# Decay matrices in place and whole head pairs in one matmul group: a state-space layer on one Trainium2 core

## The chip, the core and the metric

The kernel runs on one core of one Trainium2 chip. The time is device microseconds of that core for one execution of the whole kernel; lower is better. Engines are named as in the profile: PE multiplies matrices, DVE, ACT and POOL work elementwise, SP issues the DMAs.

## The reference

A trunk of two layers, each a feed-forward half step, a token mixer and another half step, for 512 tokens of width 1024. The change is in the mixer of the first layer, a bidirectional state-space scan in chunks (here of 128 tokens):

```python
def ssd_chunked(X, dt, A, Bm, Cm):
    Xc = (X * dt[..., None]).reshape(b, c, CHUNK, g, j, p)
    a_cs = jnp.cumsum(a, axis=-1)
    L = jnp.exp(segsum(a))
    CB = jnp.einsum('bclgn,bcsgn->bgcls', Cc, Bc)
    y_diag = jnp.einsum('bgcls,bgjcls,bcsgjp->bclgjp', CB, L, Xc)
    ...
    states = jnp.einsum('bgjzc,bcgjpn->bzgjpn', chunk_decay, states)[:, :-1]
    y_off = jnp.einsum('bclgn,bcgjpn,bgjcl->bclgjp', Cc, states, jnp.exp(a_cs))
    return (y_diag + y_off).reshape(b, t, h, p)
```

`mamba2_bidir` runs it forward and on the flipped sequence, adds both, gates with SiLU(z), normalizes by group and projects out. There are 32 heads of width 64 in 4 groups of 8 heads. In the matrix `CB * L` the forward scan fills the lower triangle and the backward scan the upper one, and the diagonal gets both.

## The kernel before

All activations lie as channels x tokens, 128 channels by 512 tokens to a tile. Float32 products of projections are split in a high and a low part (`split`: ACT makes the high part at L123, DVE the low part at L124), and three matmuls make one product (`mm3`, L166). A projection of one column tile takes 24 such matmuls of 128x512 and is called a unit here. Its 512 KB of weights come through `load` (L99), issued by SP into a ring of 4 tiles.

The state-space stage `ssm` works through four head groups. `dt_chain` computes the decay rows and writes them to a scratch array `scr` in DRAM. For a group, `prepare` makes transposes, the products CB of the two token halves (`cbs`, 256 tokens each) and the states between halves. A group has four head pairs. For a pair:

- `ssd_head`, once for a head, reads that head's decay rows of both directions into a tile `rw` (512 KB written, L744) and the decay towards the other half into `ch` (256 KB, L746). DVE multiplies `ch` by C (L747), and POOL masks the diagonal blocks by selects (L761), in `rw` in place and into `dx`.
- `ssd_mats`, for a head and a token half c, makes a decay matrix: ACT's exponentials (L769 to L772), POOL's add of the second diagonal part (L775) and DVE's product with CB (L776). The result is a tile `E` of 128x512, out of a ring of five.
- `ssd_out`, for the pair and a token half, multiplies: six matmuls of 64 columns x 256 tokens (L786) into one PSUM tile `mid`. The profile records each as two.

Between them stands the list `todo`: projections of the next group (B, C, x, z), and the output projections of the last group (`outp`). The loop runs over eight steps s, two for a pair, and does an eighth of `todo` after each. `silu` applies all SiLUs of the next group together, since each change of ACT's function set loads a table. `gated_norm` of the last group runs in two parts.

The order in which the instructions stand on each engine isn't the program's: a scheduler puts them by its own estimates of when inputs are there and buffers come free. Each engine then runs its own list strictly in order, and waits for what the head of its list needs; this holds for SP's DMAs too.

## Time and profile before

| | |
|---|---|
| Three runs | 2184.02, 2176.71 and 2184.0 us, median 2184.0 |
| Profiled execution | 2180.44 us, span 2178.6 us |
| PE busy | 2121.8 us (97%) |
| DVE busy | 1778.6 us (82%) |
| ACT busy | 1095.2 us (50%) |
| POOL busy | 155.3 us (7%) |
| Granted PE clock, mean | 0.99 |

A line of the profile names source line, engine, operation and tiles (`out<-in`); `acc`, `mid` and `ln` are PSUM tiles. In timelines the first number is the start in microseconds from the span's start, the second the duration, and a bracket at the end gives the idle time of the engine before the instruction and who ended it. In tables by stretch there stand the stretch, its length, the busy time of PE, PE's weight loads, DVE, ACT and POOL with counts, and then the granted clock, the DMA share and the GB/s. A busy PE isn't PE at its peak. The stage of the change lies between 400 and 790 us.

### The profile page before, as it was taken

The page shows a single profiled execution, that of the slowest core. Times are in us where ns is not written, and L with a number is a line of the kernel's source. Part 1 is how long each engine was busy: PE and PEld are TensorE (multiplying, and loading weights), DVE is VectorE, ACT ScalarE, POOL GpSimd, SP SyncE. Part 2 cuts the span into 40 slices and gives each one's busy share as a digit, 9 for nine tenths or more (in the row PEclk, how much of TensorE's full clock was granted, in tenths as well). Part 3 has the DMA queues.
Part 4 walks back from the last instruction along what each step waited for, and adds up shares of the span by engine and source line. Part 5 has one row for each costly group of instructions (what it writes and reads, how often), then busy time and mean ns, then how long its engine had stood idle before and what let it go on. Part 6 is the DMA issues. An engine that isn't in the chain of part 4 may idle for free.

```text
span 2178.6 us, 34176 instructions
## 1 busy us (share of the span) xinstructions
PE 2121.8 (97%) x13182; PEld 1861.4 (85%) x13182; DVE 1778.6 (82%) x3096; ACT 1095.2 (50%) x1830; POOL 155.3 (7%) x258
## 2 busy tenths in 40 slices
PE   7999999999999989999999999999999989999998
PEld 6889899866777778999999989899888878989897
DVE  6979899556766689989889998987877879859697
ACT  4424354767655547434356434343866647424353
POOL 0000000044232300000000000000111100000000
PEclk9999999999999999999999999999999999999999
DMA  9863644564535413545443273723322221323231
GB/s 322 301 212 121 219 134 152 127 178 137 158 122 155 121 68 131 198 147 196 162 136 106 98 252 104 256 91 111 98 81 78 66 78 68 125 70 116 86 110 39
DMA packets 90083, 301.19 MB, mean 138 GB/s; under 512 B 10048, under 2 KB 13504, under 8 KB 89920
## 3 DMA queue, kind: packets, MB, share of 16 engines
q1 hardware_dynamic: 88384, 294.81, 40.8%
q0 software_dynamic: 1536, 4.20, 0.9%
q8 instruction: 103, 1.69, 0.3%
q14 instruction: 60, 0.49, 0.1%
HBM read 289.53 MB, written 5.24 MB: 135 GB/s over the span
## 4 chain that ended last, share of the span: by engine, by line
PE 80%; DVE 8%; ACT 4%; issue 4%; POOL 2%; DMA 2%; POOLq 0%; ACTq 0%; SPq 0%; DVEq 0%
PE acc L166 65%; PE mid L166 9%; PE mid L786 1%; PE mid L948 1%; POOL E L775 1%; DVE raw L184 1%; PE ln L166 1%; DMA raw<-in_adaw 1%; DMA raw<-in_wdn 1%; DVE resid L320 1%; DMA raw<-in_wgu 1%; POOL dx L761 1%; PE ln L734 1%; PE ln L970 1%; DVE lo L154 0%
## 5 line engine op out<-in xcount | busy, mean ns | idle before, releaser
L166 PE MATMUL acc<-hi,wh 128*128 128x256 f32 (+1 forms) x1584 | 530.6, 336 | 9.9 <-DVE resid L370 8.7
L166 PE MATMUL acc<-hi,wl 128*128 128x256 f32 (+1 forms) x1584 | 530.5, 335 | 0.0
L166 PE MATMUL acc<-lo,wh 128*128 128x256 f32 (+1 forms) x1584 | 529.1, 335 | 0.0
L166 PE MATMUL acc<-uh,wh 128*128 128x256 f32 (+1 forms) x1160 | 391.5, 338 | 0.3 <-ACT wh L123 0.3
L166 PE MATMUL acc<-ul,wh 128*128 128x256 f32 (+1 forms) x1160 | 389.9, 336 | 0.0
L166 PE MATMUL acc<-uh,wl 128*128 128x256 f32 (+1 forms) x1160 | 389.0, 336 | 0.0
L123 ACT ACTIVATE wh<-raw 128x1024 fp32r<-128x1024 f32 (+1 forms) x210 | 212.9, 1022 | 274.0 <-DMA raw<-in_wdn 94.2
L166 PEld LDWEIGHTS acc<-hi,wh 128*128 128x128 f32 x1584 | 300.2, 190 | 46.1 <-DVE resid L370 8.3
L453 ACT ACTIVATE wh<-raw 128x1024 fp32r<-128x1024 f32 x198 | 208.8, 1059 | 256.2 <-DVE raw L463 117.8
L166 PEld LDWEIGHTS acc<-lo,wh 128*128 128x128 f32 x1584 | 300.4, 190 | 30.7 <-DVE lo L154 1.0
L166 PEld LDWEIGHTS acc<-hi,wl 128*128 128x128 f32 x1584 | 300.4, 190 | 30.1 <-issue 0.5
L124 DVE TENSOR_TENSOR wl<-raw,wh 128x1024 fp32r<-128x1024 f32 (+1 forms) x210 | 248.9, 1186 | 47.9 <-ACT wh L123 46.5
L454 DVE TENSOR_TENSOR wl<-raw,wh 128x1024 fp32r<-128x1024 f32 x198 | 241.1, 1222 | 40.2 <-ACT wh L453 39.2
L166 PEld LDWEIGHTS acc<-uh,wh 128*128 128x128 f32 x1160 | 219.3, 189 | 29.4 <-issue 6.6
L166 PEld LDWEIGHTS acc<-ul,wh 128*128 128x128 f32 x1160 | 219.4, 189 | 24.7 <-issue 3.2
L166 PEld LDWEIGHTS acc<-uh,wl 128*128 128x128 f32 x1160 | 219.3, 189 | 23.8 <-issue 2.4
L463 DVE TENSOR_TENSOR raw<-raw 128x512 f32<-128x512 f32 x264 | 181.6, 690 | 4.9
L184 DVE SCALAR_TENSOR_TENSOR raw<-raw,cond 128x1024 f32<-128x1024 f32 x144 | 174.3, 1221 | 9.6 <-DMA raw<-in_adaw 9.3
L370 DVE SCALAR_TENSOR_TENSOR resid<-acc,gv,resid 128x512 f32<-128x512 f32 (+1 forms) x172 | 112.8, 662 | 57.5 <-PE acc L166 57.3
L316 POOL TENSOR_TENSOR rr<-vr,mhalf 128x2 f32<-128x2 f32 x12 | 8.4, 697 | 1523.4 <-DVE vr L312 1523.4
L166 PE MATMUL mid<-uh,wh 128*128 128x256 f32 (+2 forms) x332 | 99.7, 301 | 0.1
L166 PE MATMUL mid<-ul,wh 128*128 128x256 f32 (+2 forms) x332 | 99.3, 300 | 0.0
(266 smaller groups left out, 3943.4 us busy)
## 6 DMA issues: line engine op xcount, KB each, us to landing
raw<-in_wgu SPq DMA_DIRECT2D x176, 512.0 KB, 4.0
raw<-in_adaw SPq DMA_DIRECT2D x144, 512.0 KB, 4.8
raw<-in_wdn SPq DMA_DIRECT2D x64, 448.0 KB, 4.1
raw<-in_win SPq DMA_DIRECT2D x40, 512.0 KB, 3.9
raw<-in_wdn SPq DMA_DIRECT2D x32, 512.0 KB, 4.5
rw<-scr SPq DMA_DIRECT2D x32, 512.0 KB, 5.4
ch<-scr SPq DMA_DIRECT2D x32, 256.0 KB, 3.6
raw<-in_wso SPq DMA_DIRECT2D x16, 512.0 KB, 3.3
```

Source lines behind the costliest of these rows:

```text
L123: nc.scalar.activation(hi[:, :n], raw, AF.Copy)
L124: nc.vector.tensor_tensor(out=lo[:, :n], in0=raw, in1=hi[:, :n].bitcast(F32), op=ALU.subtract)
L166: last = nc.tensor.matmul(o, lhsT=a, rhs=b, start=start and j == 0, stop=j == n - 1, skip_group_check=not start)
L184: nc.vector.scalar_tensor_tensor(out=raw, in0=raw, scalar=1.0, in1=cond, op0=ALU.mult, op1=ALU.mult, accum_out=mods[l][:, j : j + 1],)
L320: nc.vector.tensor_tensor(out=t, in0=t, in1=mb, op=ALU.subtract)
L370: nc.vector.scalar_tensor_tensor(out=res[d][:, a:b], in0=pd[:, a:b], scalar=gvec[n][:, d : d + 1], in1=res[d][:, a:b], op0=ALU.mult, op1=A ...
L453: nc.scalar.activation(x[0], r, AF.Copy)
L454: nc.vector.tensor_tensor(out=x[1], in0=r, in1=x[0].bitcast(F32), op=ALU.subtract)
L463: nc.vector.tensor_tensor(out=o, in0=x, in1=y, op=ALU.add)
L734: nc.tensor.matmul(pst, lhsT=bt[:, i * P : (i + 1) * P], rhs=xd, start=o == 0, stop=o == 1)
L761: nc.gpsimd.affine_select(out=o, in_=i_, pattern=[[0, 2], [sg, P]], compare_op=ALU.is_ge, fill=-1.0e30, base=0, channel_multiplier=-sg,)
L775: nc.gpsimd.tensor_tensor(out=dg, in0=dg, in1=dx[:, c], op=ALU.add)
```

## The change

Three things change. First, the `E` tiles go: exponentials, add and product work in place in `rw`, of which there are six now instead of two, and `fetch` reads the rows of a pair one pair ahead of its use. `ch` stays at three tiles. Second, the loop runs over the four pairs: both token halves' matrices of both heads are made, then a quarter of `todo` runs, then the SiLUs if they are due, and only then `ssd_out` multiplies all of the pair, 12 matmuls in one group. Third, `prepare` of the next group comes behind the last pair's products.

```diff
-NE = 5
+NRW = 6
...
-            e1, e2, e3 = (ep.tile([P, T], F32, tag="E", name="E", bufs=NE) for _ in range(3))
+            e12, e3 = (ep.tile([P, 2, T], F32, tag="rw", name="ew", bufs=NRW) for _ in range(2))
+            e1, e2, e3 = e12[:, 0, :], e12[:, 1, :], e3[:, 0, :]
...
+        rows_of = {}
+
+        def fetch(ft):
+            if ft >= 16:
+                return
+            for h in (2 * ft, 2 * ft + 1):
+                rw = ep.tile([P, 2, T], F32, tag="rw", name="rw", bufs=NRW)
+                nc.sync.dma_start(rw, scr[:, h].unsqueeze(1)[:, :, 0:2].broadcast_to([16, 8, 2, T]))
+                rows_of[h] = rw
+
         def ssd_head(h, Ct):
-            src = scr[:, h].unsqueeze(1)
-            rw = ep.tile([P, 2, T], F32, tag="rw", name="rw")
-            nc.sync.dma_start(rw, src[:, :, 0:2].broadcast_to([16, 8, 2, T]))
+            rw = rows_of.pop(h)
             ch = ep.tile([P, T], F32, tag="ch", name="ch", bufs=3)
...
         def ssd_mats(h, c, rw, dx, cbs):
-            E = ep.tile([P, T], F32, tag="E", name="E", bufs=NE)
-            i = 2 * c
-            nc.scalar.activation(E[:, :W], rw[:, 0, c * W : (c + 1) * W], AF.Exp, bias=bias[:, i, h : h + 1])
-            nc.scalar.activation(E[:, W:], rw[:, 1, c * W : (c + 1) * W], AF.Exp, bias=bias[:, i + 1, 32 + h : 33 + h])
+            i, cc = 2 * c, slice(c * W, (c + 1) * W)
+            nc.scalar.activation(rw[:, 0, cc], rw[:, 0, cc], AF.Exp, bias=bias[:, i, h : h + 1])
+            nc.scalar.activation(rw[:, 1, cc], rw[:, 1, cc], AF.Exp, bias=bias[:, i + 1, 32 + h : 33 + h])
...
-            dg = E.rearrange("p (k q) -> p k q", k=4)[:, 0:4:3, :]
+            dg = rw.rearrange("p d (k q) -> p (d k) q", k=4)[:, i : i + 6 : 5, :]
             nc.gpsimd.tensor_tensor(out=dg, in0=dg, in1=dx[:, c], op=ALU.add)
-            nc.vector.tensor_tensor(out=E, in0=E, in1=cbs[c], op=ALU.mult)
-            return E
-
-        def ssd_out(pr_, c, py, mats, chs, xt, states):
-            cc = slice(c * W, (c + 1) * W)
+            E = rw[:, :, cc]
+            nc.vector.tensor_tensor(out=E, in0=E, in1=cbs[c].rearrange("p (k q) -> p k q", k=2), op=ALU.mult)
+
+        def ssd_out(pr_, heads, py, xt, states):
             col = [slice(pr_ * P + hh * 64, pr_ * P + (hh + 1) * 64) for hh in range(2)]
-            for k in range(3):
-                for hh in range(2):
...
+            for c in range(2):
+                cc = slice(c * W, (c + 1) * W)
+                for k in range(3):
+                    for hh in range(2):
+                        rw, ch, _ = heads[hh]
+                        lhs = xt[2 * c + k][:, col[hh]] if k < 2 else states[1 - c][:, col[hh]]
+                        rhs = rw[:, k, cc] if k < 2 else ch[:, cc]
+                        nc.tensor.matmul(py[hh * 64 : (hh + 1) * 64, cc], lhsT=lhs, rhs=rhs, start=k == 0, stop=k == 2)
...
         run(units_x(0, xs)[2:])
+        fetch(0)
...
-            for s in range(8):
-                pr_, c = divmod(s, 2)
+            for pr_ in range(4):
                 ft = g * 4 + pr_
-                if c == 0:
-                    heads = [ssd_head(ft * 2 + hh, Ct) for hh in range(2)]
-                    py = acc("mid")
-                mats = [ssd_mats(ft * 2 + hh, c, heads[hh][0], heads[hh][2], cbs) for hh in range(2)]
-                ssd_out(pr_, c, py, mats, [hd[1] for hd in heads], xt, states)
...
+                fetch(ft + 1)
+                heads = [ssd_head(ft * 2 + hh, Ct) for hh in range(2)]
+                for c in range(2):
+                    for hh in range(2):
+                        ssd_mats(ft * 2 + hh, c, heads[hh][0], heads[hh][2], cbs)
...
-                while done < tot - (2 if g == NG - 1 else 0) and done < (s + 1) * tot // 8:
+                while done < tot - (2 if g == NG - 1 else 0) and done < (pr_ + 1) * tot // 4:
                     todo[done]()
                     done += 1
-                if done >= len(first) and not batched and (s >= 6 or done == tot):
+                if done >= len(first) and not batched:
                     batched = True
                     silu(zs[g] + nbc + nxs)
-                    if g < NG - 1:
-                        cur = prepare(g + 1, nxs, nbc)
+                py = acc("mid")
+                ssd_out(pr_, heads, py, xt, states)
+                nc.vector.scalar_tensor_tensor(
+                    out=xs[pr_], in0=xs[pr_], scalar=pc(C_D + ft), in1=py, op0=ALU.mult, op1=ALU.add
+                )
+            if g < NG - 1:
+                cur = prepare(g + 1, nxs, nbc)
```

The scheduler then puts much in another order. Three places show it; numbers behind names tell buffers apart. On PE, at the first head pair of group 0, before (`mid_4382` is pair 0, `acc_4705` a projection):

```order
L786 MATMUL mid_4382<-E_4438,xt_4339 64x256
L786 MATMUL mid_4382<-E_4445,xt_4339 64x256
L786 MATMUL mid_4382<-ch_4348,st_4321 64x256
L786 MATMUL mid_4382<-ch_4366,st_4321 64x256
L166 MATMUL acc_4705<-uh_3631,wh_4701 128x512
L166 MATMUL acc_4705<-ul_3632,wh_4701 128x512
```

On PE at the same place now (`mid_4479` is pair 0, `mid_4623` pair 1):

```order
L796 MATMUL mid_4479<-ch_4353,st_4324 64x256
L796 MATMUL mid_4479<-ch_4369,st_4324 64x256
L796 MATMUL mid_4623<-rw_4349,xt_4309 64x256
L796 MATMUL mid_4623<-rw_4351,xt_4309 64x256
L796 MATMUL mid_4623<-rw_4349,xt_4319 64x256
L796 MATMUL mid_4623<-rw_4351,xt_4319 64x256
```

Behind pair 0 a projection stood; now pair 1 follows at once, since the projections of pairs 0 and 1 have both moved ahead of pair 0's group. On POOL, the adds of pair 1 before (`E_4531` to `E_4593`) and what stands around them:

```order
L761 AFFINE_SELECT rw_4512<-rw_4512 128x2x128 x2
L761 AFFINE_SELECT dx_4517<-rw_4512 128x2x128 x2
L775 TENSOR_TENSOR E_4531<-E_4531,dx_4499 128x2x128
L775 TENSOR_TENSOR E_4538<-E_4538,dx_4517 128x2x128
L775 TENSOR_TENSOR E_4586<-E_4586,dx_4499 128x2x128
L775 TENSOR_TENSOR E_4593<-E_4593,dx_4517 128x2x128
L761 AFFINE_SELECT rw_4642<-rw_4642 128x2x128 x2
```

On POOL now, the adds of pair 1 (`rw_4349`, `rw_4351`; `rw_4493` is pair 2's and `rw_4637` pair 3's):

```order
L783 TENSOR_TENSOR rw_4349<-rw_4349,dx_4500 128x2x128
L783 TENSOR_TENSOR rw_4351<-rw_4351,dx_4516 128x2x128
L783 TENSOR_TENSOR rw_4349<-rw_4349,dx_4500 128x2x128
L770 AFFINE_SELECT dx_4644<-rw_4493 128x2x128 x2
L770 AFFINE_SELECT rw_4637<-rw_4637 128x2x128 x2
L783 TENSOR_TENSOR rw_4351<-rw_4351,dx_4516 128x2x128
```

The selects of the next pair stood behind all four adds; now the last add stands behind selects of pairs 2 and 3, and `rw_4637` lies in the buffer that pair 0's matrices leave. On ACT, in the preparation of group 2, before (`xt` are the transposed copies, `rw_5941` and `rw_6130` rows of pairs fetched earlier):

```order
L727 ACTIVATE xt_5794<-ln_5789 128x512
L769 ACTIVATE E_6046<-rw_5941,ssbias_3771 128x256
L770 ACTIVATE E_6046<-rw_5941,ssbias_3771 128x256
L769 ACTIVATE E_6167<-rw_6130,ssbias_3771 128x256
L770 ACTIVATE E_6167<-rw_6130,ssbias_3771 128x256
L771 ACTIVATE dx_6135<-dx_6135,ssbias_3771 128x128
L772 ACTIVATE dx_6135<-dx_6135,ssbias_3771 128x128
```

On ACT at the same place now (`rw_6097` and `rw_6099` are the rows of pair 10, two pairs ahead):

```order
L728 ACTIVATE xt_5854<-ln_5849 128x512
L778 ACTIVATE rw_6097<-rw_6097,ssbias_3771 128x256
L728 ACTIVATE xt_5864<-ln_5859 128x512
L777 ACTIVATE rw_6097<-rw_6097,ssbias_3771 128x256
L779 ACTIVATE dx_6345<-dx_6345,ssbias_3771 128x128
L780 ACTIVATE dx_6345<-dx_6345,ssbias_3771 128x128
L777 ACTIVATE rw_6099<-rw_6099,ssbias_3771 128x256
```

The second copy stood behind exponentials of rows that had been fetched during the last group; now it stands behind an exponential of rows whose buffer was read by the matmul group just ahead of the preparation.

More of the change, by code (lines that the diff above doesn't have):

```diff
@@ L738, in prepare @@
             return xt, cbs, states, Ct
+        rows_of = {}
[6 more added lines that the diff above has]
+                rows_of[h] = rw
         def ssd_head(h, Ct):
-            src = scr[:, h].unsqueeze(1)
-            rw = ep.tile([P, 2, T], F32, tag="rw", name="rw")
-            nc.sync.dma_start(rw, src[:, :, 0:2].broadcast_to([16, 8, 2, T]))
+            rw = rows_of.pop(h)
             ch = ep.tile([P, T], F32, tag="ch", name="ch", bufs=3)
-            nc.sync.dma_start(ch, src[:, :, 2].broadcast_to([16, 8, T]))
+            nc.sync.dma_start(ch, scr[:, h].unsqueeze(1)[:, :, 2].broadcast_to([16, 8, T]))
             nc.vector.tensor_tensor(out=ch, in0=ch, in1=Ct, op=ALU.mult)
@@ L773, in ssd_mats @@
             last_exp[0] = e if h < 24 else None
-            dg = E.rearrange("p (k q) -> p k q", k=4)[:, 0:4:3, :]
+            dg = rw.rearrange("p d (k q) -> p (d k) q", k=4)[:, i : i + 6 : 5, :]
             nc.gpsimd.tensor_tensor(out=dg, in0=dg, in1=dx[:, c], op=ALU.add)
-            nc.vector.tensor_tensor(out=E, in0=E, in1=cbs[c], op=ALU.mult)
-            return E
-        def ssd_out(pr_, c, py, mats, chs, xt, states):
-            cc = slice(c * W, (c + 1) * W)
+            E = rw[:, :, cc]
+            nc.vector.tensor_tensor(out=E, in0=E, in1=cbs[c].rearrange("p (k q) -> p k q", k=2), op=ALU.mult)
+        def ssd_out(pr_, heads, py, xt, states):
             col = [slice(pr_ * P + hh * 64, pr_ * P + (hh + 1) * 64) for hh in range(2)]
-            for k in range(3):
-                for hh in range(2):
-                    lhs = xt[2 * c + k][:, col[hh]] if k < 2 else states[1 - c][:, col[hh]]
-                    rhs = mats[hh][:, k * W : (k + 1) * W] if k < 2 else chs[hh][:, cc]
-                    nc.tensor.matmul(py[hh * 64 : (hh + 1) * 64, cc], lhsT=lhs, rhs=rhs, start=k == 0, stop=k == 2)
+            for c in range(2):
[6 more added lines that the diff above has]
+                        nc.tensor.matmul(py[hh * 64 : (hh + 1) * 64, cc], lhsT=lhs, rhs=rhs, start=k == 0, stop=k == 2)
         def gated_norm(g, ys, zs):
@@ L847, in ssm @@
             tot, done, batched = len(todo), 0, False
-            for s in range(8):
-                pr_, c = divmod(s, 2)
+            for pr_ in range(4):
                 ft = g * 4 + pr_
-                if c == 0:
-                    heads = [ssd_head(ft * 2 + hh, Ct) for hh in range(2)]
-                    py = acc("mid")
-                mats = [ssd_mats(ft * 2 + hh, c, heads[hh][0], heads[hh][2], cbs) for hh in range(2)]
-                ssd_out(pr_, c, py, mats, [hd[1] for hd in heads], xt, states)
-                if c == 1:
-                    nc.vector.scalar_tensor_tensor(
-                        out=xs[pr_], in0=xs[pr_], scalar=pc(C_D + ft), in1=py, op0=ALU.mult, op1=ALU.add
-                    )
-                if s == 0 and norm is not None:
+                fetch(ft + 1)
[3 more added lines that the diff above has]
+                        ssd_mats(ft * 2 + hh, c, heads[hh][0], heads[hh][2], cbs)
+                if pr_ == 0 and norm is not None:
                     rest = norm()
-                if s == 2 and norm is not None:
+                if pr_ == 1 and norm is not None:
                     yrs[g - 1] = rest()
-                while done < tot - (2 if g == NG - 1 else 0) and done < (s + 1) * tot // 8:
+                while done < tot - (2 if g == NG - 1 else 0) and done < (pr_ + 1) * tot // 4:
                     todo[done]()
                     done += 1
-                if done >= len(first) and not batched and (s >= 6 or done == tot):
+                if done >= len(first) and not batched:
                     batched = True
                     silu(zs[g] + nbc + nxs)
-                    if g < NG - 1:
-                        cur = prepare(g + 1, nxs, nbc)
+                py = acc("mid")
[5 more added lines that the diff above has]
+                cur = prepare(g + 1, nxs, nbc)
             norm = (lambda g=g, xs=xs: gated_norm(g, xs, zs[g]))
```

## The prediction

> **What bounds the kernel now.** I read the page first, then the windows of the stretch that the change touches, then the list of waits, and last the timeline of each engine there.
>
> ```profile
> span 2178.6 us, 34176 instructions
> PE 2121.8 (97%) x13182; PEld 1861.4 (85%) x13182; DVE 1778.6 (82%) x3096; ACT 1095.2 (50%) x1830; POOL 155.3 (7%) x258
> ```
>
> TensorE (PE) is the bound, so the change can only pay where PE waits, runs at a lower clock, or switches between pieces of work. It touches the state-space stage alone. The windows below cut that stage at PE's own events; the first column is the stretch, the second its length, the third PE's busy time.
>
> ```profile
> 460.76:504.48 43.72, 39.88 (x171) 24.66 (x170) 27.77 (x36) 24.54 (x60) 19.69 (x38) 0.92 0.73 203
> 504.48:551.08 46.60, 45.14 (x217) 31.04 (x215) 32.26 (x45) 37.52 (x77) 22.21 (x31) 1.00 0.42 119
> 594.30:617.19 22.89, 21.49 (x99) 14.52 (x99) 15.93 (x22) 13.26 (x29) 5.17 (x12) 1.00 0.43 129
> 695.41:718.34 22.93, 21.56 (x99) 14.54 (x99) 16.10 (x22) 13.36 (x28) 5.46 (x11) 1.00 0.42 125
> 718.34:776.15 57.81, 54.79 (x282) 40.19 (x283) 38.19 (x54) 30.02 (x59) 19.18 (x29) 0.97 0.43 132
> ```
>
> The stretches left out, 551.08 to 594.30 and 617.19 to 695.41, have PE busy for their whole length. A busy PE may still lose time, so I price the work from rows of the chain where nothing waits:
>
> ```profile
> 563.64 5.68 PE acc L166 x24
> 569.32 1.45 PE mid L786 x12
> 570.77 11.12 PE acc L166 x48
> 595.76 0.58 PE mid L786 x2
> ```
>
> A unit (24 matmuls of 128x512, one column tile of a projection) takes 11.12 / 2 = 5.56 us. A group of one token half (6 matmuls, recorded as 12) takes 1.45 us. A unit that stands alone between two groups takes 5.68, so each interruption costs 0.12 more; a group that is cut costs more too, 0.58 us for its first matmul where a twelfth part would be 0.12 to 0.24.
>
> By these prices the first stretch (head group 0, pairs 1 to 3) holds 4 units and 6 half groups: 22.2 + 8.7 = 30.9 us of work in 43.72 us. That loses 12.8 us. The second has 5 units and 4 half groups, 33.6, and 13.0 us for the preparation of group 1 and one norm. The third and fourth have 2 units and one half group, 12.6, so that a preparation (transposes, CB products, states) costs 10.3 us each. The last has 161 unit matmuls (37.3) and 8 half groups (11.6): 8.9 us for two norms and the waits at the end. Who makes PE wait, over the whole stage:
>
> ```profile
> PE mid L786 <- DVE E L776: 3.8, 3, 3.3
> PE ln L734 <- DVE xd L730: 3.8, 4, 1.4
> PE ln L800 <- DVE gss L797: 2.2, 1, 2.2
> PE mid L786 <- DVE ch L747: 0.8, 1, 0.8
> ```
>
> **The change, part by part.** The number of instructions on every engine and of DMAs stays the same; the arithmetic is the same too. So the sum is made of waits and of interruptions.
>
> *First stretch, +1.4 us.* Pair 0 ends at 460.76, as now: everything up to it stands in the same order on PE.
>
> ```profile
> 458.02 1.08 PE L786 MATMUL mid<-E,xt 128*64 128x256 f32 x8
> 460.76 0.51 PE L166 MATMUL acc<-uh,wh 128*128 128x512 f32 x1
> 476.55 0.39 PE L166 MATMUL acc<-uh,wh 128*128 128x512 f32 x1
> 480.22 1.08 PE L786 MATMUL mid<-E,xt 128*64 128x256 f32 x2 [3.29 <-DVE E L776]
> 481.24 0.80 PE L166 MATMUL acc<-ul,wh 128*128 128x512 f32 x1
> 449.01 1.91 SPq L744 DMA_DIRECT2D rw<-scr  x2
> 454.00 1.36 POOL L761 TENSOR_SCALAR_AFFINE_SELECT rw<-rw 128x256 f32<-128x256 f32 x2 [1.78 <-DMA rw<-scr]
> 460.86 1.16 SPq L746 DMA_DIRECT2D ch<-scr  x2
> 464.06 1.08 DVE L747 TENSOR_TENSOR ch<-ch,xc 128x512 f32<-128x512 f32 x1 [0.44 <-DMA ch<-scr]
> 464.14 1.73 SPq L744 DMA_DIRECT2D rw<-scr  x2
> 474.27 0.77 POOL L761 TENSOR_SCALAR_AFFINE_SELECT rw<-rw 128x256 f32<-128x256 f32 x2 [7.94 <-DMA rw<-scr]
> 465.07 0.68 DVE L776 TENSOR_TENSOR E<-E,cb 128x512 f32<-128x512 f32 x1
> 461.80 0.74 POOL L775 TENSOR_TENSOR E<-E,dx 128x256 f32<-128x256 f32 x1 [0.65 <-ACT dx L772]
> ```
>
> In the changed order pair 1's group follows pair 0's at once, with no projection between them. The rows rw of pair 1 are fetched early, but its second ch is not: there are still three ch tiles, so that DMA is issued when pair 0's group has read its own ch, and on DVE the multiplication by it stands ahead of the two products of pair 1. From issue to use takes 464.06 - 460.86 = 3.2 us, then 1.08 and 0.68: PE starts pair 1 at 465.8, after 5.0 us of idling. Its last four matmuls need an add on POOL that stands behind the selects of pair 3's rows; those come into pair 0's buffers, so their DMA also waits for pair 0's group: issued at 461.4, 5.0 us to the first select (449.01 to 454.00), then 0.77, 0.74 and 0.68: 468.6. Pair 2 has ACT's exponentials, POOL's adds and a ch behind three weight loads ahead of it, and its products share DVE with the weight split for the next unit; step by step by these prices PE has pair 1 done at 471.5, begins pair 2 at 473.6, and is back at whole units at 478.0. From there 44 matmuls (10.2), a rest of pair 2 (0.5), two units (11.1) and pair 3 (2.7) remain, and 3.4 us for the clock, below: 505.9, or 45.1 us where now 43.7 pass. Both orders lose about 13 us here: what the old one lost in pieces (the 3.29 us wait, a clock of 0.73, cut groups) the new one loses in one block.
>
> The clock: after the wait of 3.29 us a matmul that took 0.39 us takes 0.80. The granted clock (the third number from the right) is short of full by 0.27 and 0.07 of 10 us in the next two windows, 3.4 us lost, or 6.8 us at half speed.
>
> ```profile
> 475.00:485.00 10.00, 6.71 (x23) 3.28 (x21) 6.31 (x10) 7.85 (x19) 5.17 (x11) 0.73 0.85 209
> 485.00:495.00 10.00, 9.84 (x41) 6.28 (x40) 5.18 (x9) 6.79 (x17) 7.00 (x12) 0.93 0.38 114
> ```
>
> The longer wait of 5.0 us should do the same, so I keep 3.4. The Trainium skill, "TensorE: Matmul & The Clock Gate", section "Part 1: The HAM clock gate", speaks against this change too: an idle window of about 3.4 us halves the clock, and about 3.4 us of sustained work restores it. By its figure the loss after the block would be estimated at 1.7 us and the whole sum at -11.6 instead of -9.9. This case's trace agrees on the halving (3.29 us), and has the return only after 6.8 us.
>
> Ends: -2 if the clock recovers during the broken matmuls of pairs 1 and 2 (no loss behind them); +7 if the second DMA lands like the one issued at 464.14, 10.1 us before its select, because weights are ahead of it. I stay near the 5.0, as here it follows one ch only.
>
> *Start of group 1, -2.5 us.* The 13.0 us contain one norm, which PE pays with 0.98 and 0.97:
>
> ```profile
> 719.78 0.98 PE ln L800 x8
> 775.18 0.97 PE ln L253 x4
> ```
>
> That leaves 11.0 for the preparation. In the new order three units are spread between its steps, the exponentials of pairs 0 and 1 stand before the SiLUs, and no group is cut into it. Following the order, xd of the first and second chunk come 0.9 and 0.7 us late (the ACT copies stand behind exponentials on rows just fetched), other waits are under 0.5: 8.5 us. Ends -5 (no wait at all) and +2 (that fetch at 10.1).
>
> *Start of groups 2 and 3, -1.4 us each.* PE now has one group of 12, then the preparation without any group in it, and 48 matmuls of projections between the steps. One wait is new: the second transposed copy on ACT stands behind an exponential on pair 10's rows, whose DMA waits for the group just multiplied.
>
> ```profile
> rw<-scr SPq DMA_DIRECT2D x32, 512.0 KB, 5.4
> L769 ACT ACTIVATE E<-rw,ssbias 128x256 f32<-128x256 f32 x64 | 32.0, 499 | 18.1 <-POOL rw L761 17.6
> L727 ACT ACTIVATE xt<-ln 128x512 f32<-128x512 f32 x16 | 9.5, 593 | 7.3 <-PE ln L725 7.3
> ```
>
> From the end of that group: issue of a ch 0.6 (half of 1.16), the rows' median to landing 5.4, three selects 1.2 (two take 0.77), exponential 0.5, copy 0.6: 8.3 us, while PE gets there after 6.6 and waits 1.7. With the later copies I count 20.0 us for 2 units and preparation, 8.9 for the latter against 10.3. Ends -3 and +4 each: the same DMA at 10.1 adds 5.
>
> *End of group 3, -3.5 us.* Now the last pair's decay matrices come after the four SiLUs of z and a second table load:
>
> ```profile
> 756.35 2.19 ACT z L696 x4
> 758.55 1.28 ACT L769
> 762.22 1.29 POOL E L775
> 769.62 0.67 DVE xc L857
> ```
>
> and PE waits 2.2 us for the norm, 0.8 for ch, and runs its small pieces apart: 8.9 - 3.9 for two norms = 5.0 lost. In the new order pair 3's matrices are ready before pair 2's group. Its last ch is issued when pair 2 has read its own, behind a 512 KB weight load, and 13 matmuls (3.0 us) cover it: some 1.4 us of waiting, and 0.6 for the norm's power on POOL. Gain 3.0, and the first pairs' waits bring it to 3.5. Ends -6 and 0.
>
> *One group for one pair, -2.5 us.* Pair 0 already runs as one group in the trace: 458.02 to 460.76 is 2.74, against 2 x 1.45 = 2.90. With the interruption saved, 0.28 a pair. I count it for 9 pairs, not for group 0 or the pairs whose cut is counted above. Ends 0 and -3.4 (12 pairs).
>
> The early fetch of pair 0 and the six row tiles are free: SP's first weight load behind it is needed on ACT only at 474. If that cover went, a unit would come 4 to 5 us late.
>
> Sum: 1.4 - 2.5 - 2.8 - 3.5 - 2.5 = -9.9 us. The profiled execution took 2180.44 us (span 2178.6), so 2170.5. The runs shown are 2184.02, 2176.71 and 2184.0, with mean 2181.6; a median of new runs stands 1 to 3 us above the profiled one, so I say 2172, 12 us (0.55%) under the median shown.
>
> **The rivals.**
>
> *The gain is given back at the row fetch (no change).* The rows for two pairs ahead now wait for PE, not for ACT, and the engines' orders put their users ahead of urgent work. For it: the 7.94 us wait above. Against it: later fetches have 3 or 4 units, 17 to 22 us, ahead of them. With two of four such fetches at 10.1 us instead of 5: -10 + 10, so about 2182.
>
> *Slower.* One mechanism: every one of these fetches lands behind weight loads, at 10 us, and each wait grows past the 3.3 us after which the clock halves the clock. Place: pair 1 of group 0 and the three starts. Price: 5 + 3.4 at each of the four, 34 us, on -10: +24, or 2206. It passes +0.5% once all four land after 8.5 us or later. Against it: on the queue a ch alone stands ahead of these fetches in three of four places.
>
> *The block in group 0 does not come.* If ch lands sooner and the clock stays up, the first stretch gains 6 us instead of losing 1: about 2164. Against it: three ch tiles are unchanged, so the DMA cannot start sooner.
>
> **How the numbers follow.** Forecast 0.50 (2165 to 2178), given back 0.33 (2177 to 2190), slower 0.10, no block 0.07. About 0.5%, 11 us, is what a measurement of this kernel can tell from no change: the line is at 2173 and 2195. Of the forecast three quarters lie under 2173, with the last case 0.45 for faster; the rest and the second case give 0.45; slower 0.10. All terms at their good ends give -22, at their bad ends +17; not all go one way, so I take 2161 to 2187, which leaves out the slower case and a little on either side.
>
> **What would show it.** In the new trace: pair 1's group about 5 us behind pair 0's, with DVE ch as its releaser; granted clock under 1 between 465 and 485; the stretch to the end of pair 3 at 44 to 46 us; the starts of groups 2 and 3 at 20 to 21.5 us, with ACT's second copy late behind a DMA of rows; no wait of 2 us for gss. The prediction is wrong if the first stretch takes over 50 us, or if weight loads on SP come late because ch holds the queue.

## Result and profile after

The changed kernel took 2191.97 us (median of 6 runs, 2190.0 to 2196.76), the kernel before 2181.6 us (6 runs). The ratio is 1.0054, with a 95% interval of 1.0043 to 1.0064: slower by 10 us, where 12 us faster was forecast, and outside the forecast range of 2161 to 2187. The profiled execution of the changed kernel is the slowest of its six, 2196.76 us.

The page after, span and engines:

```profile
span 2195.0 us, 34153 instructions
PE 2120.8 (97%) x13182; PEld 1866.2 (85%) x13182; DVE 1784.5 (81%) x3096; ACT 1094.5 (50%) x1830; POOL 167.4 (8%) x258
```

PE has the same work and the span is 16 us longer, so the time went into waits. To place them I cut the stage of the change at marks that every version has on PE: the first matmul of a head pair's group, the last state matmul of the preparations of groups 1, 2 and 3, and the matmul of L274 behind the stage. Windows of the kernel before, between these marks (stretch, length, PE's busy time, PE's weight loads, DVE, ACT, POOL, granted clock, DMA share, GB/s):

```profile
458.02:530.20 72.18, 66.99 (x301) 43.19 (x301) 44.19 (x58) 50.76 (x112) 31.35 (x51) 0.95 0.59 162
530.20:612.20 82.00, 80.49 (x388) 58.45 (x387) 58.27 (x78) 53.12 (x106) 28.28 (x47) 1.00 0.47 140
612.20:713.30 101.10, 99.73 (x481) 74.76 (x480) 66.25 (x86) 59.38 (x114) 29.57 (x49) 1.00 0.45 136
713.30:788.29 74.99, 71.97 (x358) 54.05 (x356) 53.45 (x76) 38.28 (x72) 19.18 (x29) 0.98 0.39 122
```

The same of the changed kernel:

```profile
457.95:535.70 77.75, 61.89 (x286) 41.99 (x286) 50.84 (x64) 54.04 (x119) 41.74 (x58) 0.93 0.54 159
535.70:633.60 97.90, 94.83 (x458) 71.94 (x458) 64.88 (x84) 56.75 (x110) 31.80 (x48) 0.98 0.47 136
633.60:736.30 102.70, 99.35 (x481) 75.93 (x481) 67.58 (x87) 58.40 (x113) 31.33 (x49) 0.98 0.46 134
736.30:799.43 63.13, 59.57 (x310) 44.95 (x308) 44.30 (x63) 28.97 (x49) 11.62 (x15) 0.97 0.35 106
```

Length less busy time is PE's idle time: 5.2, 1.5, 1.4 and 3.0 us before, 15.9, 3.1, 3.4 and 3.6 us after, 14.8 us more in all, and the clock is lower in every stretch. The stage begins at the same time (458.02 and 457.95) and ends 11.1 us later (788.29, 799.43). The other 5 us of the profiled execution lie behind the stage, where nothing was changed; the medians, 10 us apart, leave no room for them. Who makes PE wait in the stage:

```profile
PE mid L796 <- DVE rw L785: 5.7, 2, 4.5
PE ln L726 <- ACT xt L728: 5.0, 2, 2.5
PE mid L796 <- DVE ch L756: 4.5, 2, 2.4
PE mid L796 <- issue: 3.0, 1, 3.0
PE ln L705 <- ACT xc L697: 3.0, 1, 3.0
PE ln L735 <- DVE xd L731: 2.8, 4, 1.7
```

L796 is the pair's group; L705, L726 and L735 belong to the preparation, and their waits, 10.8 us, were 4.1 before. How they come about is seen at the start of group 2 (timeline; L748 reads rows, L770 selects, L778 is an exponential, L728 the preparation's transposed copy):

```profile
613.50 1.19 SPq L748 DMA_DIRECT2D rw<-scr  x2
620.31 0.76 POOL L770 TENSOR_SCALAR_AFFINE_SELECT rw<-rw 128x256 f32<-128x256 f32 x2 [15.03 <-DMA rw<-scr]
621.46 0.51 ACT L778 ACTIVATE rw<-rw,ssbias 128x256 f32<-128x256 f32 x1 [5.07 <-POOL dx L770]
621.88 0.58 ACT L728 ACTIVATE xt<-ln 128x512 f32<-128x512 f32 x1
622.51 0.77 PE L726 MATMUL ln<-csts,xc 128*128 128x128 f32 x4 [2.43 <-ACT xt L728]
```

PE's group ends at 612.80 and frees its row tiles. The rows of pair 10 are issued at 613.50 and are there at 620.3. On ACT an exponential on them stands ahead of the copy that PE needs next, so ACT idles 5.07 us and PE 2.43. The exponential could have waited: pair 10's group stands at 688.42 in this trace, 67 us later.

Group 0 has the same on two queues. Before, SP and ACT (weights are `raw` on SP, `wh` on ACT):

```profile
437.46 1.54 SPq L99 DMA_DIRECT2D raw<-in_win  x3
451.48 2.04 ACT L123 ACTIVATE wh<-raw 128x1024 fp32r<-128x1024 f32 x2
457.90 1.06 ACT L123 ACTIVATE wh<-raw 128x1024 fp32r<-128x1024 f32 x1 [4.38 <-PE acc L166]
```

After:

```profile
440.06 0.36 SPq L99 DMA_DIRECT2D raw<-in_win  x1
460.78 0.51 SPq L755 DMA_DIRECT2D ch<-scr  x1
461.39 1.19 SPq L748 DMA_DIRECT2D rw<-scr  x2
463.27 2.00 SPq L99 DMA_DIRECT2D raw<-in_win  x3
470.46 0.51 ACT L777 ACTIVATE rw<-rw,ssbias 128x256 f32<-128x256 f32 x1 [9.09 <-POOL dx L770]
474.62 1.99 ACT L123 ACTIVATE wh<-raw 128x1024 fp32r<-128x1024 f32 x2
```

A ch that waits for PE's first group (458 to 460.8) holds up SP, so the weights behind it are issued at 463.27 instead of 437.46. On ACT their split stands behind twelve exponentials whose rows waited for the same group, and comes at 474.62 instead of 451.48 and 457.90. PE has little but the pairs' groups in that time, and waits for those.

### The profile page after: what moved, and what is told of

The parts are those of the page before. It is cut to its first block, busy times and chain, and to the rows that moved or that the text cites. A ratio compares the mean times of both kernels' runs of the same rounds, so it can differ in the third digit from the quotient of the medians.

```text
span 2195.0 us, 34153 instructions
## 1 busy us (share of the span) xinstructions
PE 2120.8 (97%) x13182; PEld 1866.2 (85%) x13182; DVE 1784.5 (81%) x3096; ACT 1094.5 (50%) x1830; POOL 167.4 (8%) x258
## 4 chain that ended last, share of the span: by engine, by line
PE 75%; DVE 11%; DMA 5%; ACT 4%; issue 2%; POOL 1%; SPq 0%; POOLq 0%; ACTq 0%; DVEq 0%
PE acc L166 61%; PE mid L166 8%; DMA rw<-scr 2%; PE mid L796 1%; DVE raw L184 1%; DVE raw L463 1%; DMA raw<-in_adaw 1%; DVE wl L124 1%; PE mid L959 1%; DVE wl L454 1%; DMA raw<-in_wdn 1%; PE ln L166 1%; DMA raw<-in_wgu 1%; PE ln L735 1%; DMA ch<-scr 1%
## 5 line engine op out<-in xcount | busy, mean ns | idle before, releaser
L166 PEld LDWEIGHTS acc<-lo,wh 128*128 128x128 f32 x1584 | 301.8, 191 | 31.6 <-DVE lo L154 1.3
L166 PE MATMUL mid<-uh,wl 128*128 128x256 f32 (+2 forms) x332 | 99.5, 300 | 0.0
```

The source lines that it names most:

```text
L166: last = nc.tensor.matmul(o, lhsT=a, rhs=b, start=start and j == 0, stop=j == n - 1, skip_group_check=not start)
```

## Experiments

Three theories. Theory 1: work on tiles that PE's group has just freed is put ahead of urgent work on engines that run in order, and holds it up. Theory 2: the merged group and the place of the preparation cost the time by themselves. Theory 3: the three ch tiles do. Each run has five rounds, and its ratio is to runs of the kernel before on the same chip. That kernel's medians lie between 2178.8 and 2181.6 us on these chips, so times of two runs can differ by 3 us for that alone; the ratios don't have this. As a second reading I give for each the loss in the four stretches above: their length less 0.2317 us (5.56 / 24) for each projection matmul and 0.2283 us (2.74 / 12) for each of a pair's matmuls that PE's order has between the marks. A projection matmul of 256 columns counts half; in seven kernels 6 or 15 of them stand at the end of the last stretch, the others have none there. A preparation, the norms, waits and lost clock remain in it. It is from the one profiled execution of each kernel; those of order_only and ch_four lie 6.6 and 5.9 us under their medians, so there the table holds only part of the difference.

| kernel | median us | ratio, 95% interval | losses in the four stretches, us | sum |
|---|---|---|---|---|
| before | 2181.6 | 1 | 23.4, 13.8, 12.3, 9.3 | 58.9 |
| after | 2191.97 | 1.0054 (1.0043 to 1.0064) | 31.6, 14.4, 13.9, 9.1 | 69.0 |
| order_only | 2193.76 | 1.0063 (1.0050 to 1.0077) | 23.5, 14.9, 14.2, 13.4 | 66.0 |
| rows_only | 2190.37 | 1.0047 (1.0035 to 1.0059) | 25.2, 18.8, 15.6, 4.9 | 64.5 |
| copies_first | 2186.54 | 1.0035 (1.0021 to 1.0048) | 30.4, 10.3, 11.0, 10.3 | 61.9 |
| ch_four | 2191.88 | 1.0055 (1.0043 to 1.0067) | 31.6, 13.8, 12.5, 4.1 | 62.1 |
| spread_group0 | 2190.11 | 1.0047 (1.0030 to 1.0065) | 29.0, 14.8, 13.9, 9.6 | 67.2 |
| prepare_inside | 2191.46 | 1.0055 (1.0043 to 1.0067) | 30.5, 13.3, 12.5, 10.3 | 66.6 |
| rows_copies | 2182.86 | 1.0011 (1.0002 to 1.0019) | 22.0, 11.1, 13.2, 13.1 | 59.4 |
| combined | 2185.63 | 1.0032 (1.0021 to 1.0044) | 30.6, 13.8, 10.7, 8.2 | 63.4 |
| prep_first | 2178.14 | 0.9988 (0.9979 to 0.9997) | 25.3, 9.8, 9.5, 8.4 | 53.0 |
| prep_first_group0 | 2176.32 | 0.9985 (0.9976 to 0.9993) | 22.5, 9.8, 9.4, 9.5 | 51.2 |
| halves_repaired | 2184.13 | 1.0017 (1.0008 to 1.0026) | 23.5, 10.3, 15.5, 12.2 | 61.5 |
| order_prep_first | 2180.24 | 1.0002 (0.9993 to 1.0011) | 25.2, 11.4, 9.3, 16.2 | 62.2 |
| prep_first_three_ch | 2180.16 | 0.9996 (0.9987 to 1.0004) | 24.6, 11.1, 9.3, 14.6 | 59.7 |
| before_prep_first | 2189.52 | 1.0034 (1.0022 to 1.0046) | 20.8, 11.8, 14.4, 19.0 | 65.9 |
| own_weights | 2171.34 | 0.9947 (0.9933 to 0.9961) | 17.3, 10.2, 9.1, 9.0 | 45.6 |

### The two halves of the change apart

order_only: the new loop with the old tiles, of which E has eight now instead of five. The edit is shown against the changed kernel.

```diff
-NRW = 6
+NE = 8
...
-                fetch(ft + 1)
...
-                for c in range(2):
-                    for hh in range(2):
-                        ssd_mats(ft * 2 + hh, c, heads[hh][0], heads[hh][2], cbs)
+                mats = [[ssd_mats(ft * 2 + hh, c, heads[hh][0], heads[hh][2], cbs) for hh in range(2)] for c in range(2)]
```

> The kernel before with only the second half of the change: both token halves of a pair in one group behind the pair's projections, preparation behind the last pair. The decay matrices still go into tiles E (8 instead of 5, so that a pair's four and the next pair's four find room), and the rows are fetched at the head of their own pair into two tiles that ACT frees. Theory 1 (the early fetch into tiles that PE frees, with ACT's exponentials on them ahead of the copies of the preparation, costs the time): no such wait here, the starts of groups 2 and 3 at 20 to 21 us, no block in group 0; 2176 to 2182 us. Theory 2 (the moved preparation and the merged group cost it): about the changed kernel, 2188 to 2194 us. Theory 3 (the three ch tiles cost it, since one group now holds two of them for its whole length): 2184 to 2188 us with the ch waits of 4.5 and 2.1 us in place.

Measured 2193.76 us, ratio 1.0063. Theory 1 as it stood here, tied to the early fetch, is wrong: the order alone loses as much as the whole change. Theory 2's range has it. PE's waits name the same victims, xd and xc of the preparation, though no rows are fetched a pair ahead:

```profile
PE ln L734 <- DVE xd L730: 7.8, 6, 3.2
PE mid L786 <- DVE ch L747: 5.9, 1, 5.9
PE ln L704 <- ACT xc L696: 2.9, 1, 2.9
```

The start of group 2 shows how (timeline of SP and ACT; L761 selects, L771 is an exponential, L727 the transposed copy):

```profile
605.68 1.52 SPq L744 DMA_DIRECT2D rw<-scr  x2
614.31 0.40 ACT L771 ACTIVATE dx<-dx,ssbias 128x128 f32<-128x128 f32 x1 [2.68 <-POOL dx L761]
617.34 0.59 ACT L727 ACTIVATE xt<-ln 128x512 f32<-128x512 f32 x1
```

ACT idles 2.68 us for selects on rows issued at 605.68, and a copy of the preparation stands behind exponentials on them. PE then waits 3.06 us for the xd made from that copy. These rows come into tiles that ACT frees, so theory 1 has to be taken wider: work whose input is still on its way stands ahead of urgent work on an engine that runs in order, whoever freed the tile.

rows_only: the new tiles and fetch in the old loop of eight half steps.

```diff
-            for pr_ in range(4):
+            for s in range(8):
+                pr_, c = divmod(s, 2)
...
+                if c == 0:
+                    fetch(ft + 1)
...
-                ssd_out(pr_, heads, py, xt, states)
+                ssd_out(pr_, heads, py, xt, states, (c,))
```

> The kernel before with only the first half of the change: decay matrices made in place in six row tiles, rows fetched one pair ahead. The loop of eight half steps stays, with the preparation inside the last pair. Theory 1: slower than before, 2186 to 2194 us, with PE waiting in the preparations for a copy behind an exponential on rows just fetched, and a block of group matmuls in group 0. Theory 2: about before, 2179 to 2184 us. Theory 3: 2179 to 2186 us, since each group of a half frees nothing later than before.

Measured 2190.37 us, ratio 1.0047: as theory 1 has it. The two halves don't add up (1.0063 and 1.0047, together 1.0054), so each alone loses about what both lose, in its own way.

### One edit each to the changed kernel

copies_first:

```diff
+            if h % 8 >= 4:
+                for x in es:
+                    tc.add_manual_dep(x.ins, last_xt[0].ins.name, NOSYNC, reason="transposed copies first")
```

`es` are the four exponentials of `ssd_mats`; the dependency orders ACT's list and adds no wait of its own.

> The changed kernel, with ACT's exponentials of the third and fourth pair of each group ordered behind the four transposed copies xt of that group's preparation; nothing else. Theory 1: PE no longer waits in the preparations for xt, the starts of groups 2 and 3 fall from about 24 to 20 or 21 us and that of group 1 by 2 to 4; 2180 to 2186 us. Theory 2: the copies were late only for lack of cover; 1 or 2 us at most, 2188 to 2193 us. Theory 3: the ch waits stay, 2188 to 2193 us.

Measured 2186.54 us, ratio 1.0035: a little above theory 1's range and below theory 2's by the median, and 2189 us, in theory 2's, by the ratio (1.0035 x 2181.6). The interval just overlaps the changed kernel's, so this run decides little by its time. The waits for xt are gone from the list, and the second and third stretch lose 4.1 and 2.9 us less; the wait for xc ahead of the preparation of group 1 is longer instead, 5.5 us for 3.0.

ch_four: `bufs=4` for `ch`.

> The changed kernel with four ch tiles instead of three, so that both of a pair's ch can be fetched while the pair ahead is multiplied. Theory 1: the ch waits of 4.5 us in group 0 and 2.1 us in group 3 go, in group 0 part of it comes back as a wait for rows; 2187 to 2192 us. Theory 2: the same, 2187 to 2192 us. Theory 3: 2181 to 2186 us.

Measured 2191.88 us, ratio 1.0055, no change, so theory 3 falls. The waits for ch are gone, as theory 1 had it, and the time is the same.

spread_group0: units 2, 3, 2 and 1 to the pairs of group 0, dependencies that put each group behind its own units, and those of pairs 2 and 3 behind the weights emitted before them.

```diff
-                while done < tot - (2 if g == NG - 1 else 0) and done < (pr_ + 1) * tot // 4:
+                while done < tot - (2 if g == NG - 1 else 0) and done < ((2, 5, 7, 8)[pr_] if g == 0 else (pr_ + 1) * tot // 4):
...
+                        if behind:
+                            tc.add_manual_dep(m.ins, last_mm[0].ins.name, NOSYNC, reason="behind the projections")
```

> The changed kernel with group 0 alone put in another order: the four pairs take 2, 3, 2 and 1 units instead of 2 each, each pair's group stands behind its own units, and the rows and exponentials of pairs 2 and 3 stand behind the weights of those units on SP and ACT. On PE the groups of group 0 then stand one by one, with 1, 2 and 1 units between them, where the changed kernel has two and a half of them in a row. Theory 1 (the block of group 0 costs 7 to 8 us, which the losses by stretch of the traces so far show): 2183 to 2187 us, with the loss from the first group to the end of the second preparation at 24 us instead of 31.6. Theory 2 (what group 0 loses it loses in any order, in one block or in pieces, as the prediction had it): 2189 to 2193 us.

Measured 2190.11 us, ratio 1.0047, not to be told from the changed kernel and in theory 2's range. Theory 1's number here was wrong: taking the block of groups apart gains nothing, since PE now waits for weights behind the first group instead, 12.1 us in one wait for wl.

prepare_inside: `cur = prepare(g + 1, nxs, nbc)` moved back behind `silu`, ahead of the last pair's `ssd_out`.

> The changed kernel with the preparation of the next head group put back ahead of the last pair's group, where it stood before; rows, tiles and merged groups as changed. Theory 1 (exponentials on rows just fetched stand ahead of the copies, wherever the preparation is): 2188 to 2194 us. Theory 2 (the place of the preparation costs the time): 2180 to 2186 us, with the starts of groups 2 and 3 back at 21 us.

Measured 2191.46 us, ratio 1.0055. The place of the preparation isn't the cause: that part of theory 2 falls.

### Repairs put together

rows_copies: rows_only with the edit of copies_first.

> The run with the rows alone (eight half steps, rows in place, six tiles), with ACT's exponentials of the third and fourth pair behind the preparation's four copies. Theory 1: the losses of the second and third stretch fall from 18.8 and 15.6 us by 4 to 6 and 3 to 4, the block of group 0 stays: 2181 to 2185 us. Theory 2 (cutting the groups into halves between the steps of the preparation is what costs there): 2187 to 2191 us.

Measured 2182.86 us, ratio 1.0011: of the 0.47% that rows_only lost, 0.36 is given back by one engine's order. That is in theory 1's range, for that half.

combined: copies_first (from the second pair on), ch_four and spread_group0.

> The changed kernel with all three repairs: group 0 spread as in the run of that name, the exponentials of the second, third and fourth pair behind the preparation's copies, four ch tiles. Theory 1 (the losses of the stretches add up: 24 + 10.3 + 11.0 + 4.1 us, against 58.9 in the kernel before): 2168 to 2174 us, faster than before. Theory 2 (what a stretch gains is lost again in the next, since PE only meets the weights sooner): 2178 to 2186 us.

Measured 2185.63 us, ratio 1.0032: in theory 2's range, and theory 1's sum was wrong by 13 us. The trace shows why. Timeline of PE and DVE, where L738 is the states' matmul, L761 the product with ch and L734 the product xd:

```profile
471.97 0.79 PE L168 MATMUL acc<-uh,wl 128*128 128x512 f32 x1 [11.04 <-DVE wl L126]
517.43 0.81 DVE L761 TENSOR_TENSOR ch<-ch,xc 128x512 f32<-128x512 f32 x1 [5.44 <-DMA ch<-scr]
518.16 0.68 DVE L734 TENSOR_TENSOR xd<-xt,dd 128x512 f32<-128x512 f32 x1
518.89 2.08 PE L738 MATMUL ln<-xd,bt 128*128 128x512 f32 x2 [5.74 <-DVE xd L734]
```

I had put ACT's list in order and left DVE's: there a product with a ch that is still on its way stands ahead of xd, and PE waits 5.74 us. In group 0 the split of a weight (wl, 470.37) stands behind pair 1's products with CB, the last of which comes at 467.13 after 3.33 us of waiting for an add on POOL, and PE waits 11.04 us.

prep_first: the changed kernel with four ch tiles, and ACT's and DVE's work for the second to fourth pair behind the preparation.

```diff
+            if h % 8 >= 2:
+                for x in es:
+                    tc.add_manual_dep(x.ins, last_xt[0].ins.name, NOSYNC, reason="transposed copies first")
...
+            if h % 8 >= 2:
+                tc.add_manual_dep(v.ins, last_xd[0].ins.name, NOSYNC, reason="preparation first")
```

`v` is DVE's product with ch, and that with CB.

> The changed kernel with four ch tiles, and with all that ACT and DVE do for the second to fourth pair of a group (exponentials, products with ch, products with the CB tile) ordered behind the copies xt and the products xd of that group's preparation; group 0 before its last pair as changed. Theory 1 (the time goes where work on tiles that PE has just freed stands ahead of the preparation on an in-order engine): no wait for xt, xd or xc of more than 1.5 us, losses by stretch about 28, 10, 11 and 4 to 8 us, 53 to 57 in all against 58.9 before: 2176 to 2182 us. Theory 2 (a preparation behind the last pair's group has nothing to cover it, whatever the order): 2185 to 2190 us.

Measured 2178.14 us, ratio 0.9988: 14 us less than the changed kernel, in theory 1's range. All waits of the preparation that are left in its list:

```profile
PE ln L735 <- DVE xd L731: 0.3, 1, 0.3
```

order_prep_first: the same dependencies in order_only.

> The order_only run (tiles E, merged groups, preparation behind the last pair), with ACT's and DVE's work for the second to fourth pair of a group behind the preparation's copies xt and products xd. Theory 1: the waits for xd (7.8 us) and xc (2.9 us) go, that for ch (5.9 us) stays: 2183 to 2187 us. Theory 2: 2190 to 2194 us.

Measured 2180.24 us, ratio 1.0002: 13.5 us less than order_only, and less than theory 1's range. By its time the order on ACT and DVE gives back what that half lost, and theory 2 falls with it. The traces place only part of it: the waits for xd (7.8 us) are gone, those for xc (3.8) and ch (5.3) stand, and the profiled runs lose 62.2 and 66.0 us.

prep_first_group0: prep_first and spread_group0, with DVE's products of pairs 2 and 3 behind wl too.

> As prep_first, and in group 0 the weights first on all three engines: units 2, 3, 2 and 1 to a pair, each group behind its own units, rows fetched behind these units' loads on SP, and exponentials and products of pairs 2 and 3 behind the units' splits on ACT and DVE. Theory 1: the wait of 11 us for wl that the combined run had in group 0 does not come, the first stretch loses 22 to 26 us: 2172 to 2178 us. Theory 2: 2183 to 2188 us. If pair 1's products still hold up a split, 2178 to 2183 us.

Measured 2176.32 us, ratio 0.9985, in theory 1's range but not to be told from prep_first. What was to go is only split up: PE still waits 10.3 us for wl in the stage, in three waits, the longest 6.2.

halves_repaired: rows_copies with DVE's order and four ch tiles.

> The rows_copies run (eight half steps, rows in place in six tiles, exponentials of the third and fourth pair behind the copies), with the products of those pairs on DVE behind the preparation as well and four ch tiles. Both theories: the 5.1 us that PE waited there for ch fall to 1 or 2, 2177 to 2181 us, no slower than before; theory 2 has it faster than prep_first, theory 1 within 3 us of it.

Measured 2184.13 us, ratio 1.0017: a miss for both theories. The next section returns to it.

### What was still open

prep_first_three_ch: prep_first with three ch tiles.

> prep_first with the three ch tiles of the changed kernel, so that the order of ACT and DVE behind the preparation is the only edit to the changed kernel. If the order alone accounts for the loss: 2178 to 2182 us. If the fourth ch tile did half of it: 2184 to 2187 us.

Measured 2180.16 us, ratio 0.9996. This is the changed kernel with dependencies alone added, and the order gives back 0.58 of a per cent, all that the change had lost; the fourth tile's share (0.9988 against 0.9996) lies within the intervals. The scheduler also moves some projection matmuls on PE: 43 instead of 39 stand between the last state matmul of group 2 and the next group.

before_prep_first: the kernel before with the same dependencies.

> The kernel before with the same order of ACT and DVE (second to fourth pair behind the preparation's copies xt and products xd), all else as before. If the loss belongs to the change, since only its early fetch and later release let such work run ahead: 2177 to 2181 us, not more than 0.1% from before. If the kernel before lost as much at its preparations: 2168 to 2174 us.

Measured 2189.52 us, ratio 1.0034, slower, which neither case had. So the rule is no gain for every kernel; it helps the changed one and hurts this one. That the kernel before had nothing of this loss doesn't follow: its waits for xd (3.8 us) are gone here, and the first two stretches lose 2.6 and 2.0 us less, but the third loses 2.1 and the last 9.7 us more. What PE waits for now:

```profile
PE mid L796 <- DVE E L784: 9.1, 9, 3.4
```

Nine waits of a half step's group for its matrices, where the old order had three of 3.8 us in all. In the last stretch PE idles 6.9 us instead of 3.0, at a granted clock of 0.94 instead of 0.98. In its order on PE a half step's group follows the last state matmul after 5 or 12 projection matmuls, 1.2 to 2.8 us by 0.2317, so its matrices have little cover when they are put off; in prep_first the merged group follows after 19 to 43, 4.4 to 10 us. That fits halves_repaired as well, which has the same 5 and 12; that it is the reason was not tried apart in either.

own_weights: prep_first_group0, with group 0's units emitted ahead of the rows of their pair, so that on SP their loads stand ahead of the ch and rows that wait for PE.

```diff
+                while g == 0 and done < (2, 5, 7, 8)[pr_]:
+                    todo[done]()
+                    done += 1
+                fetch(ft + 1)
                 heads = [ssd_head(ft * 2 + hh, Ct) for hh in range(2)]
```

> prep_first_group0, with a pair's units of group 0 written ahead of its rows, so that on SP the loads of pair 2's and 3's own units stand ahead of their ch and rows, which wait for PE. If SP's order is what still holds up the weights in group 0: the waits for wl (10.3 us in two places) fall to 3 us or less, the first stretch loses 17 to 19 us instead of 22.5: 2170 to 2174 us. If DVE's order is, 2175 to 2178 us.

Measured 2171.34 us, ratio 0.9947 (0.9933 to 0.9961): as expected if SP's order is what held up the weights, and faster than both kernels, some 20 us under the changed one. Windows between the same marks:

```profile
457.47:518.40 60.93, 55.51 (x275) 39.57 (x275) 45.76 (x57) 45.31 (x97) 42.17 (x54) 0.94 0.65 182
518.40:613.70 95.30, 95.07 (x465) 72.22 (x465) 67.04 (x86) 56.84 (x113) 35.35 (x49) 1.00 0.50 138
613.70:711.60 97.90, 97.85 (x481) 75.00 (x480) 64.88 (x87) 57.59 (x114) 35.33 (x49) 1.00 0.46 140
711.60:774.37 62.77, 59.20 (x305) 44.40 (x305) 52.47 (x73) 40.71 (x82) 21.86 (x26) 0.97 0.36 107
```

PE idles 0.2 and 0.1 us in the second and third stretch, with a preparation in each. In the first, three weight loads are issued ahead of the rows that wait for PE's first group, where the changed kernel had one and the next at 463.27 (timeline of SP):

```profile
435.55 1.51 SPq L99 DMA_DIRECT2D raw<-in_win  x1
444.35 1.59 SPq L99 DMA_DIRECT2D raw<-in_win  x2
459.87 1.16 SPq L751 DMA_DIRECT2D rw<-scr  x2
461.13 1.19 SPq L760 DMA_DIRECT2D ch<-scr  x2
462.37 2.00 SPq L99 DMA_DIRECT2D raw<-in_win  x2
```

PE's waits for wl fall from 10.3 to 4.4 us, not quite to the 3 expected.

## Why the prediction was wrong, step by step

The forecast's sum was -9.9 us; by the marks of the two traces the stage became 11.1 us longer. Two steps failed: the waits at the starts of groups 1, 2 and 3 were priced too low, which is most of the difference, and the early fetch was put at nothing.

- *First stretch, forecast +1.4, measured +3.1.* Pair 3's group ends at 507.54, 46.8 us behind 460.76. The block, the wait at pair 1 (4.53 us, 5.0 forecast, put down to the product that stands behind the late ch on DVE) and 3.4 us lost to the clock came as worked out, the last in two spells (granted clock 0.83 from 460 to 470 and 0.85 from 480 to 490) and not in one. Units began at 482.0 instead of 478.0. The step that failed is "The early fetch of pair 0 and the six row tiles are free": the weight load behind them was issued 26 us later than before, and its cover was gone. That is the sign of being wrong that the prediction itself named, weight loads late because ch holds the queue; it had the right price for a unit, 4 to 5 us, and left it out of the sum.
- *Start of group 1, forecast -2.5, measured +3.7.* From 507.54 to the end of the norm are 36.4 us for three units and pair 0; two units and pair 1 at 13.9 make 50.3, against 46.6. I forecast late xd of 0.9 and 0.7; one came 1.68 late, and before it PE waited 3.01 us for a SiLU that stands behind exponentials on ACT. The prediction names that order and puts all such waits under 0.5.
- *Starts of groups 2 and 3, forecast -1.4 each, measured +2.8 and +2.2* (24.2 us from 612.80 and 23.7 from 715.92, for 20.0 forecast and, less the half group of 1.45, 21.4 and 21.5 before). The place was named, ACT's second copy behind an exponential on pair 10's rows, with a wait of 1.7 us; it was 2.43 and 2.53. What the sum left out: the rows were there 6.8 us after issue, not 5.4, and 1.7 us went to the halved clock, below. Small waits (in group 2 for xd, 0.2 and 0.5, and for the norm, 0.4) are part of the rest. The two rivals had this mechanism too, at +10 and +34 on the sum; the three starts together came out 14.1 us over the forecast for them.
- *End of group 3, forecast -3.5.* The wait of 2.2 us for gss went, as forecast; 2.08 us for ch and 1.46 for the norm's power came, 1.4 and 0.6 forecast. The last stretch, 9.1 us for 9.3, loses only 0.2 us less than before.
- *One group for one pair, forecast -2.5.* The merged groups take 2.74 us wherever nothing waits, so the price stands. Between the starts, where both kernels keep PE busy, the stretches to 594.30 and 695.41 before, to 612.80 and 715.92 now, lose 0.9 and 0.7 us less by the prices of the table.

The measured terms, 3.1 + 3.7 + 2.8 + 2.2 - 0.2 - 0.9 - 0.7 = 10.0 us, and 0.7 us for six half matmuls that now stand ahead of the last mark make up the 11.1 us within half a microsecond. So the forecast had the right mechanism, work on freshly fetched rows ahead of urgent work, named it at some of the places, priced it too low at each, and gave its slow end 1 in 10. The step under all of them: I priced a wait by what is waited for, and not by what stands queued behind it on its engine. The second and third stretch show what the merged groups are worth without that: 9.8 and 9.5 us of loss in prep_first, for 13.8 and 12.3 before, or 11.8 and 12.3 if the better of before and before_prep_first is taken. With SP's order mended in group 0 as well the kernel stands 10 us under the median before, what I had forecast for the change as it stood; that the number is the same is chance, since it comes with other edits.

What stays open: why order_only's median lies 6.6 us over its profiled run, and how the 20 us between the changed kernel and own_weights divide among SP, ACT and DVE in group 0, since the three were put in order together. Group 0's new order was not tried on the kernel before, so how much of the 10 us under it is owed to the change itself isn't shown either.

## What to carry to other kernels

When a buffer's release moves to a later reader, follow everything that the scheduler can now place between release and use: on an in-order engine an instruction on a tile that is just being refilled holds up all behind it for the whole landing time of its DMA. Take from the order of each engine, SP included, what stands directly behind each such instruction and who waits for that. The remedy was not a buffer (a fourth ch tile changed nothing) but an order: urgent small work (copies, splits, weight loads) ahead of work for the pair after next, on all engines at once, since ACT's order alone left the wait to DVE. It doesn't pay everywhere: it made the kernel before slower, perhaps because the work put off has less cover there, which wasn't tried.

## What the hardware showed that I had not expected

The clock falls after shorter waits than I allowed for. I took the 3.29 us wait of the trace before as what it takes. In the changed kernel's windows of 10 us, one at each of the three preparations,

```profile
510.00:520.00 10.00, 6.99 (x28) 5.63 (x28) 7.04 (x12) 8.42 (x16) 2.19 (x5) 0.83 0.71 210
620.00:630.00 10.00, 7.38 (x25) 4.71 (x25) 5.30 (x7) 6.71 (x16) 6.33 (x10) 0.83 0.15 39
720.00:730.00 10.00, 7.47 (x27) 4.78 (x27) 7.26 (x11) 4.21 (x11) 4.99 (x9) 0.83 0.39 109
```

the granted clock is short by 0.17, 1.7 us or 3.4 us at half speed, around waits of 3.01, 2.43 and 2.53 us. In the kernel before, the windows with the preparations of groups 2 and 3 have 1.00:

```profile
600.00:610.00 10.00, 8.60 (x38) 5.53 (x37) 5.75 (x9) 5.19 (x14) 3.78 (x9) 1.00 0.37 110
700.00:710.00 10.00, 8.63 (x35) 5.33 (x34) 7.03 (x10) 5.58 (x15) 4.76 (x10) 1.00 0.43 125
```

PE's longest waits there are 1.40 and 1.28 us. Each of these three preparations paid 1.7 us on top of its wait. The Trainium skill, "TensorE: Matmul & The Clock Gate", section "Part 1: The HAM clock gate", gives a window of about 3.4 us of idling and as much of work to come back. The trace agrees with the way back, 3.4 us at half speed each time, and the 6.8 us that I read in the trace before are twice that. With the way down it differs: no PE wait in those three windows reaches 3.4 us.

The DMAs of rows land later in the changed kernel. The page's median from issue to landing for `rw<-scr` went from 5.4 to 7.4 us:

```profile
rw<-scr SPq DMA_DIRECT2D x32, 512.0 KB, 7.4
```

From group 1 on SP issued the rows of a pair's two heads some 6 us apart or more before (594.37 and 600.17 at the start of group 2). Now it issues them one behind the other, right after PE's group; the first lands 5.2 to 7.0 us after issue and the second 7.1 to 8.1. So the later landing goes with the bunch; that the bunch is its cause no run shows.
